# A softmax over 32768 columns: stores moved to ScalarE's queue, fixed buffers and a hand-written order

## The chip, the cores and the metric

The kernel runs on one core of one Trainium2 chip. The metric is the time of one execution on the device, in microseconds (us). Several executions of each kernel are timed and the median is given; one more execution is recorded by the hardware profiler, and all views of the profile are of that one. Names used below: VectorE is DVE in the profile, ScalarE is ACT, SyncE is SP (SPq where it issues transfers), GpSimd is POOL. TensorE has no work here.

## The reference

```python
def setup_inputs():
    batch, seq, vocab = 16, 256, 32768
    return {
        "logits": np.random.randn(batch, seq, vocab).astype(np.float32),
        "temperature": 1.0,
    }

def reference(logits, temperature):
    scaled = logits / temperature
    scaled = scaled - scaled.max(axis=-1, keepdims=True)
    exp_scaled = np.exp(scaled)
    return (exp_scaled / exp_scaled.sum(axis=-1, keepdims=True)).astype(np.float32)
```

It is a softmax over the last axis of a 4096 x 32768 float32 matrix. 536.87 MB are read and 536.87 MB are written, and each element needs to be read once and written once.

## The kernel before

Each of the 4096 rows is cut in two halves of 16384 columns (`_SPLIT = 2`), and each half is given a partition. A tile is therefore 128 partitions x 16384 float32: 64 rows of the matrix, 64 KB per partition, 8.39 MB. There are `G` = 64 tiles, contiguous in memory. `CW` equals the half row, so a tile is one chunk (`C` = 1) and the chunk index `i` is the tile index.

Three tile buffers (`_BUFS = 3`) come from a pool. For one tile the work is this:

- `load(i)`: SyncE issues a transfer from memory into the buffer. Tiles 0 and 63 are loaded in four transfers of 16 KB per partition, all others in one of 64 KB (line 64).
- `exps(i)`: for each of four pieces of 4096 columns, VectorE takes the negated maximum (line 107) and ScalarE computes Exp in place with that maximum as bias and a running sum (line 114).
- `factors(g)`: a few instructions on columns of 1 to 4 elements turn the four maxima and sums of each partition, and those of the partition with the other half of the same row (a shuffle, line 84), into one factor per piece (lines 129 to 150). They are marked as high priority.
- `scales(i)`: for each piece VectorE multiplies the first 2560 columns by the factor (line 160), and ScalarE multiplies the other 1536 (line 163).
- `store(i)`: SyncE issues the transfer back to memory, one of 64 KB per partition, or four of 16 KB for tile 63 (line 75).

All transfers thus go through one queue, SyncE's, and they are kept in program order. That order is written out by hand:

```python
    order = [("L", i) for i in range(min(_BUFS, n_chunks))] + [("S", 0)]
    for i in range(1, n_chunks):
        order.append(("S", i))
        if i + _BUFS - 1 < n_chunks:
            order.append(("L", i + _BUFS - 1))
```

SyncE's sequence is load 0, 1, 2, store 0, store 1, load 3, store 2, load 4, and so on. A store waits for the scaling of its tile by both engines. A load into a buffer waits for the store that empties it, and, because SyncE works in order, it also stands behind the store that precedes it in this sequence. A transfer is split over 16 DMA engines, 8 partitions to each, so that in a whole-tile transfer each engine moves eight rows of 64 KB.

Of the kernel before, what the change touches and what calls it, by code (L numbers as in the profile page):

```python
# [6 lines left out]


_SPLIT = 2
_CW = 16384  # L10
_BUFS = 3
_PIECE = 4096
_LAST_DMA = 4096
_DVE_SHARE = 0.625


@with_exitstack
def kernel(
    ctx: ExitStack,
    tc: tile.TileContext,  # L20
    logits: bass.AP,
    temperature: bass.AP,
    out: bass.AP,
):
    nc = tc.nc
    inv_t = 1.0 / float(temperature)
    P = nc.NUM_PARTITIONS
    fp32 = mybir.dt.float32
    Exp = mybir.ActivationFunctionType.Exp
    Copy = mybir.ActivationFunctionType.Copy  # L30
    X = mybir.AxisListType.X
    A = mybir.AluOpType

    xf = logits.flatten_outer_dims()
    of = out.flatten_outer_dims()
    N, V = xf.shape
    W = V // _SPLIT
    CW = min(_CW, W)
    C = W // CW
    assert W * _SPLIT == V and CW * C == W and (N * _SPLIT) % P == 0  # L40
    x = xf.rearrange("n (h v) -> (n h) v", h=_SPLIT)
    o = of.rearrange("n (h v) -> (n h) v", h=_SPLIT)
    G = N * _SPLIT // P
    n_chunks = G * C
    n_rounds = _SPLIT.bit_length() - 1

    xpool = ctx.enter_context(tc.tile_pool(name="x", bufs=_BUFS))
    spool = ctx.enter_context(tc.tile_pool(name="stats", bufs=3))
    slots = {}
    stats = {}  # L50

    def spans(total: int, step: int) -> list[tuple[int, int]]:
        return [(s, min(step, total - s)) for s in range(0, total, step)]

    def piece(g: int) -> int:
        return _PIECE if g < G - 1 else min(_PIECE, _LAST_DMA)

    def load(i: int) -> None:
        g, c = divmod(i, C)
        xs = xpool.tile([P, CW], fp32, tag="x", name="xs")  # L60
        slots[i] = xs
        for s, n in spans(CW, _LAST_DMA if g in (0, G - 1) else CW):
            tc.keep_in_program_order(
                nc.sync.dma_start(
                    out=xs[:, s : s + n],
                    in_=x[g * P : (g + 1) * P, c * CW + s : c * CW + s + n],
                )
            )

    def store(i: int) -> None:  # L70
        g, c = divmod(i, C)
        xs = slots.pop(i)
        for s, n in spans(CW, _LAST_DMA if g == G - 1 else CW):
            tc.keep_in_program_order(
                nc.sync.dma_start(  # L75
                    out=o[g * P : (g + 1) * P, c * CW + s : c * CW + s + n],
                    in_=xs[:, s : s + n],
                )
            )

    def combine(v, op) -> None:
        for j in range(n_rounds):
            mask = [i ^ (1 << j) for i in range(32)]
            nc.vector.stream_shuffle(  # L84
                out=v[:, j + 1 : j + 2], in_=v[:, j : j + 1], mask=mask
            )
            nc.vector.tensor_tensor(  # L87
                out=v[:, j + 1 : j + 2],
                in0=v[:, j : j + 1],
                in1=v[:, j + 1 : j + 2],  # L90
                op=op,
            )

    def exps(i: int) -> None:
        g, c = divmod(i, C)
        xs = slots[i]
        ps = spans(CW, piece(g))
        K = C * len(ps)
        if c == 0:
            stats[g] = tuple(  # L100
                spool.tile([P, K], fp32, tag=f"{nm}{K}", name=nm)
                for nm in ("nm", "ssum", "ee", "f", "ttj")
            )
        nm, ssum = stats[g][:2]
        for j, (s, n) in enumerate(ps):
            k = c * len(ps) + j
            nc.vector.tensor_reduce(  # L107
                out=nm[:, k : k + 1], in_=xs[:, s : s + n], axis=X, op=A.max, negate=True
            )
            if inv_t != 1.0:  # L110
                nc.vector.tensor_scalar_mul(
                    out=nm[:, k : k + 1], in0=nm[:, k : k + 1], scalar1=inv_t
                )
            nc.scalar.activation(  # L114
                out=xs[:, s : s + n],
                in_=xs[:, s : s + n],
                func=Exp,
                bias=nm[:, k : k + 1],
                scale=inv_t,
                accum_out=ssum[:, k : k + 1],  # L120
            )

    def factors(g: int) -> None:
        nm, ssum, ee, f, ttj = stats[g]
        nMh = spool.tile([P, 1 + n_rounds], fp32, tag="nMh", name="nMh")
        Sh = spool.tile([P, 1 + n_rounds], fp32, tag="Sh", name="Sh")
        rS = spool.tile([P, 1], fp32, tag="rS", name="rS")
        with tc.high_priority():
            nc.vector.tensor_reduce(out=nMh[:, 0:1], in_=nm, axis=X, op=A.min)  # L129
            combine(nMh, A.min)  # L130
            nc.scalar.activation(  # L131
                out=ee,
                in_=nm,
                func=Exp,
                bias=nMh[:, n_rounds : n_rounds + 1],
                scale=-1.0,
            )
            nc.vector.tensor_tensor_reduce(  # L138
                out=ttj,
                in0=ee,  # L140
                in1=ssum,
                scale=1.0,
                scalar=0.0,
                op0=A.mult,
                op1=A.add,
                accum_out=Sh[:, 0:1],
            )
            combine(Sh, A.add)
            nc.vector.reciprocal(out=rS, in_=Sh[:, n_rounds : n_rounds + 1])  # L149
            nc.vector.tensor_scalar_mul(out=f, in0=ee, scalar1=rS)  # L150

    def scales(i: int) -> None:
        g, c = divmod(i, C)
        xs = slots[i]
        f = stats[g][3]
        ps = spans(CW, piece(g))
        for j, (s, n) in enumerate(ps):
            k = c * len(ps) + j
            cut = int(n * _DVE_SHARE) // 512 * 512
            nc.vector.tensor_scalar_mul(  # L160
                out=xs[:, s : s + cut], in0=xs[:, s : s + cut], scalar1=f[:, k : k + 1]
            )
            nc.scalar.activation(  # L163
                out=xs[:, s + cut : s + n],
                in_=xs[:, s + cut : s + n],
                func=Copy,
                scale=f[:, k : k + 1],
            )

    order = [("L", i) for i in range(min(_BUFS, n_chunks))] + [("S", 0)]  # L170
    for i in range(1, n_chunks):
        order.append(("S", i))
        if i + _BUFS - 1 < n_chunks:
            order.append(("L", i + _BUFS - 1))

    nxt = 0
    done = -1
    loaded = 0
    for kind, i in order:
        if kind == "L":  # L180
            load(i)
            loaded = i + 1
        else:
            g = i // C
            if g > done:
                while nxt < (g + 1) * C:
                    assert nxt < loaded
                    exps(nxt)
                    nxt += 1
                factors(g)  # L190
                done = g
            scales(i)
            store(i)


# [33 lines left out]
```

## Time and profile before

| | |
|---|---|
| median of 8 runs | 2503.75 us (2497.48 to 2507.66) |
| the profiled execution | 2505.58 us, of which the span is 2503.8 us |
| VectorE busy | 1579.6 us (63%), 1216 instructions |
| ScalarE busy | 1368.8 us (55%), 833 instructions |
| DMA | 1073.91 MB in 19748 packets, mean 429 GB/s |
| maximum of 4096 columns, VectorE (line 107) | 256 times, mean 4412 ns |
| Exp of 4096 columns, ScalarE (line 114) | 256 times, mean 3708 ns |
| scaling, VectorE 2560 columns (line 160) | 256 times, mean 1549 ns |
| scaling, ScalarE 1536 columns (line 163) | 256 times, mean 1564 ns |

The span runs from the first to the last instruction in the trace. The busy shares are averages over it. "Issue to landing" of a transfer, used below, counts from the instruction that issues it to the moment its data are known to be there; it includes the time in which the transfer is queued behind others.

### The profile page before, as it was taken

How to read it: one execution, taken by the hardware profiler on the slowest of the kernel's cores; microseconds unless marked ns; L12 is line 12 of the kernel's file. 1: busy time of each engine (PE TensorE's matmuls, PEld its weight loads, DVE VectorE, ACT ScalarE, POOL GpSimd, SP SyncE). 2: the span in 40 equal slices, each digit the busy share in tenths (PEclk: the TensorE clock that was granted, in tenths of full speed). 3: DMA queues.
4: the chain of work that ended last, by engine and by line, in shares of the span. 5: the costliest groups of instructions: out<-in, count | busy, mean ns of one | idle time of the engine just before them, and what ended most of it. 6: DMA issues, size and time to landing. Idle time of an engine off the chain costs nothing.

```text
span 2503.8 us, 2498 instructions
## 1 busy us (share of the span) xinstructions
DVE 1579.6 (63%) x1216; ACT 1368.8 (55%) x833; POOL 0.2 (0%) x4
## 2 busy tenths in 40 slices
DVE  6575665765656657666575665766657566576665
ACT  5464554645546456465564655546556465564655
POOL 0000000000000000000000000000000000000000
DMA  9999999999999999999999999999999999999998
GB/s 419 434 427 428 435 433 435 435 436 431 436 436 435 429 434 429 435 434 433 433 423 433 424 431 433 424 421 436 429 425 433 431 423 435 420 435 432 423 425 376
DMA packets 19748, 1073.91 MB, mean 429 GB/s; under 512 B 2192, under 2 KB 2192, under 8 KB 2192
## 3 DMA queue, kind: packets, MB, share of 16 engines
q1 hardware_dynamic: 19728, 1073.75, 99.8%
q14 instruction: 20, 0.16, 0.0%
HBM read 536.87 MB, written 536.87 MB: 429 GB/s over the span
## 4 chain that ended last, share of the span: by engine, by line
DMA 71%; DVE 16%; ACT 10%; another core or an unknown queue 1%; SPq 1%; issue 0%; ACTq 0%
DMA xs<-in_logits_dram 69%; DVE nm L107 14%; ACT xs L163 7%; ACT xs L114 3%; DMA out_dram<-xs 2%; DVE xs L160 1%; SPq L75 1%; DVE f L150 0%; ACT ee L131 0%; DVE rS L149 0%; DVE Sh L87 0%; DVE Sh L84 0%; DVE ttj L138 0%; ACTq L224 0%
## 5 line engine op out<-in xcount | busy, mean ns | idle before, releaser
L107 DVE TENSOR_REDUCE nm<-xs 128x1 f32<-128x4096 f32 x256 | 1113.7, 4412 | 661.0 <-DMA xs<-in_logits_dram 661.0
L114 ACT ACTIVATE xs<-xs,nm 128x4096 f32<-128x4096 f32 x256 | 949.2, 3708 | 1032.1 <-DVE nm L107 1032.1
L163 ACT ACTIVATE xs<-xs,f 128x1536 f32<-128x1536 f32 x256 | 382.3, 1564 | 73.5 <-DVE f L150 73.5
L160 DVE TENSOR_SCALAR xs<-xs,f 128x2560 f32<-128x2560 f32 x256 | 380.2, 1549 | 2.6 <-DVE f L150 0.4
L138 DVE CUSTOM_DVE_ANT_0 ttj<-ee,ssum 128x4 f32<-128x4 f32 x64 | 10.4, 162 | 222.5 <-ACT ee L131 222.5
L114 ACT ACTIVATION_READ_ACCUMULATOR xs<-xs,nm 128x1 f32 x256 | 47.9, 187 | 0.0
L131 ACT ACTIVATE ee<-nm,nMh 128x4 f32<-128x4 f32 x64 | 18.0, 282 | 0.0
L150 DVE TENSOR_SCALAR f<-ee,rS 128x4 f32<-128x4 f32 x64 | 14.7, 229 | 2.2
L149 DVE RECIPROCAL rS<-Sh 128x1 f32<-128x1 f32 x64 | 10.5, 164 | 2.2
L87 DVE TENSOR_TENSOR nMh<-nMh 128x1 f32<-128x1 f32 x64 | 10.2, 159 | 2.2
L87 DVE TENSOR_TENSOR Sh<-Sh 128x1 f32<-128x1 f32 x64 | 10.2, 159 | 2.2
L129 DVE TENSOR_REDUCE nMh<-nm 128x1 f32<-128x4 f32 x64 | 10.0, 157 | 2.2
L84 DVE STREAM_SHUFFLE nMh<-nMh 128x1 f32<-128x1 f32 x64 | 9.7, 151 | 0.0
L84 DVE STREAM_SHUFFLE Sh<-Sh 128x1 f32<-128x1 f32 x64 | 9.7, 151 | 0.0
L114 ACT ACT_TABLE_LOAD x1 | 1.3, 1283 | 8.0 <-DMA xs<-in_logits_dram 8.0
L138 DVE DVE_READ_ACCUMULATOR2_ANT Sh<- 128x1 f32 x64 | 5.3, 82 | 0.0
L84 DVE LOAD_MASK_SELECT nMh<-nMh x64 | 0.9, 14 | 2.8
L84 DVE LOAD_MASK_SELECT Sh<-Sh x64 | 0.9, 14 | 2.8
L210 POOL MEMSET const-bfloat16-1.0<- 128x1 bf16 x1 | 0.1, 102 | 0.0
L210 POOL MEMSET const-uint8-127<- 128x1 uint8 x1 | 0.1, 102 | 0.0
L210 POOL MEMSET const-float32-0.0<- 128x1 f32 x1 | 0.1, 99 | 0.2 <-issue 0.2
L210 POOL MEMSET const-float32-1.0<- 128x1 f32 x1 | 0.1, 99 | 0.0
## 6 DMA issues: line engine op xcount, KB each, us to landing
xs<-in_logits_dram SPq DMA_DIRECT2D x8, 2048.0 KB, 27.6
out_dram<-xs SPq DMA_DIRECT2D x4, 2048.0 KB, 15.4
out_dram<-xs SPq DMA_DIRECT2D x63, 29.6
xs<-in_logits_dram SPq DMA_DIRECT2D x62, 49.2
```

The costliest lines, as they stand in the source:

```text
L75: nc.sync.dma_start(out=o[g * P : (g + 1) * P, c * CW + s : c * CW + s + n], in_=xs[:, s : s + n],)
L84: nc.vector.stream_shuffle(out=v[:, j + 1 : j + 2], in_=v[:, j : j + 1], mask=mask)
L87: nc.vector.tensor_tensor(out=v[:, j + 1 : j + 2], in0=v[:, j : j + 1], in1=v[:, j + 1 : j + 2], op=op,)
L107: nc.vector.tensor_reduce(out=nm[:, k : k + 1], in_=xs[:, s : s + n], axis=X, op=A.max, negate=True)
L114: nc.scalar.activation(out=xs[:, s : s + n], in_=xs[:, s : s + n], func=Exp, bias=nm[:, k : k + 1], scale=inv_t, accum_out=ssum[:, k : k + 1],
L129: nc.vector.tensor_reduce(out=nMh[:, 0:1], in_=nm, axis=X, op=A.min)
L131: nc.scalar.activation(out=ee, in_=nm, func=Exp, bias=nMh[:, n_rounds : n_rounds + 1], scale=-1.0,)
L138: nc.vector.tensor_tensor_reduce(out=ttj, in0=ee, in1=ssum, scale=1.0, scalar=0.0, op0=A.mult, op1=A.add, accum_out=Sh[:, 0:1],)
L149: nc.vector.reciprocal(out=rS, in_=Sh[:, n_rounds : n_rounds + 1])
L150: nc.vector.tensor_scalar_mul(out=f, in0=ee, scalar1=rS)
L160: nc.vector.tensor_scalar_mul(out=xs[:, s : s + cut], in0=xs[:, s : s + cut], scalar1=f[:, k : k + 1])
L163: nc.scalar.activation(out=xs[:, s + cut : s + n], in_=xs[:, s + cut : s + n], func=Copy, scale=f[:, k : k + 1],)
```

## The change

The kernel is written anew around the same arithmetic.

- The three tile buffers and three sets of small statistics tiles are allocated once and used in turn, tile `t` in buffer `t % 3`, in place of pools.
- Each engine executes its instructions in the order of the program (`tc.manual_schedule()`). The high-priority section is gone.
- Tiles 1 to 62 are computed in five pieces of 4096, 4096, 4096, 2048 and 2048 columns. VectorE scales 4096, 4096 and 2048 columns of the first three pieces, and ScalarE the remaining 2048 of the third and the last two pieces whole. Tiles 0 and 63 keep four pieces of 4096, with 2560 columns scaled by VectorE.
- Stores are issued by ScalarE, on its own queue: one transfer of 64 KB per partition after the scaling of a tile, and for tile 63 one of 16 KB per partition after each piece.
- Loads stay with SyncE. The load of tile `t + 3` follows the computation of tile `t` in the program, and waits for the store of tile `t`. Its size is `_LOAD` elements.

```diff
-_CW = 16384
 _BUFS = 3
-_PIECE = 4096
-_LAST_DMA = 4096
-_DVE_SHARE = 0.625
+_LOAD = 16384
+_PIECES = (4096, 4096, 4096, 2048, 2048)
+_ON_DVE = (4096, 4096, 2048, 0, 0)
+_END = 4096
+_END_ON_DVE = 2560
+_SETS = 3
...
+    pool = ctx.enter_context(tc.tile_pool(name="fixed", bufs=1))
+    buf = [pool.tile([P, W], fp32, tag=f"x{b}", name=f"x{b}") for b in range(_BUFS)]
...
+    def load(t: int) -> None:
+        n = _END if t in (0, G - 1) else _LOAD
+        for s in range(0, W, n):
+            nc.sync.dma_start(
+                out=buf[t % _BUFS][:, s : s + n],
+                in_=x[t * P : (t + 1) * P, s : s + n],
             )
...
-                nc.sync.dma_start(
-                    out=o[g * P : (g + 1) * P, c * CW + s : c * CW + s + n],
-                    in_=xs[:, s : s + n],
-                )
-            )
+    def store(t: int, a: int, b: int) -> None:
+        nc.scalar.dma_start(
+            out=o[t * P : (t + 1) * P, a:b], in_=buf[t % _BUFS][:, a:b]
+        )
...
+        for k in range(K):
+            a, b, c = at[k], at[k] + on_dve[k], at[k] + sizes[k]
+            if b > a:
+                nc.vector.tensor_scalar_mul(
+                    out=xs[:, a:b], in0=xs[:, a:b], scalar1=f[:, k : k + 1]
+                )
+            if c > b:
+                nc.scalar.activation(
+                    out=xs[:, b:c], in_=xs[:, b:c], func=Copy, scale=f[:, k : k + 1]
+                )
+            if t == G - 1:
+                store(t, a, c)
+        if t < G - 1:
+            store(t, 0, W)
...
-        with tc.high_priority():
-            nc.vector.tensor_reduce(out=nMh[:, 0:1], in_=nm, axis=X, op=A.min)
...
+    with tc.manual_schedule():
+        for t in range(_BUFS):
+            load(t)
+        for t in range(G):
+            normalise(t)
+            if t + _BUFS < G:
+                load(t + _BUFS)
```

The loop over pieces with the maxima and Exps, and the instructions for the factors, are the same as before with the new piece sizes and stand in `normalise(t)` in the same order.

## The prediction

> **What bounds the kernel now.** I read the page from the top: the DMA row and the rates under it, then the chain, the waits, SyncE's own waits, and last the timeline of SyncE's issues.
>
> ```profile
> DMA  9999999999999999999999999999999999999998
> GB/s 419 434 427 428 435 433 435 435 436 431 436 436 435 429 434 429 435 434 433 433 423 433 424 431 433 424 421 436 429 425 433 431 423 435 420 435 432 423 425 376
> ...
> q1 hardware_dynamic: 19728, 1073.75, 99.8%
> ...
> DMA 71%; DVE 16%; ACT 10%; another core or an unknown queue 1%; SPq 1%; issue 0%; ACTq 0%
> ...
> out_dram<-xs SPq DMA_DIRECT2D x63, 29.6
> xs<-in_logits_dram SPq DMA_DIRECT2D x62, 49.2
> ```
>
> The 16 DMA engines are busy for 99.8% of the span, all on one queue (q1, SyncE's). The best slices reach 436 GB/s, the worst in the middle 420; only the first and last are low for want of work. The chain is 71% DMA. So the bytes bound the kernel: 1073.74 MB, which the change does not touch. What can move is the rate at which they pass, and the two ends.
>
> ```profile
> DVE nm L107 <- DMA xs<-in_logits_dram: 661.0, 65, 22.9
> ```
>
> ```profile
> SPq L75 <- DVE xs L160: 2383.8, 67, 39.2
> ```
>
> VectorE waits 661 us for loads, so computing has room. SyncE stands 2383.8 us before its stores, waiting for VectorE's scaling; the next load is queued behind that wait. The waits end in time, because the queue holds work meanwhile:
>
> ```profile
> 385.63 0.33 SPq L75 DMA_DIRECT2D out_dram<-xs  x1
> 386.01 0.43 SPq L64 DMA_DIRECT2D xs<-in_logits_dram  x1
> 424.27 0.33 SPq L75 DMA_DIRECT2D out_dram<-xs  x1
> 424.65 0.43 SPq L64 DMA_DIRECT2D xs<-in_logits_dram  x1
> 462.93 0.33 SPq L75 DMA_DIRECT2D out_dram<-xs  x1
> ```
>
> Store and load go out as a pair, once a period. From the fourth store (150.25) to the last whole one (2454.01) are 59 periods in 2303.76 us, 39.05 us each. The shortest, and the commonest, is 38.63 us: two tiles of 8.39 MB at 434 GB/s. The other periods are up to 1.5 us longer. Over the 59 this costs 2303.8 - 59 x 38.63 = **24.6 us**, the only reserve inside the loop. The trace's packet records show where it lies: of the 16,000 rows of 64 KB, 95 in 100 took 2.415 to 2.427 us and none less; the slow ones, up to 3.9 us, sit almost all at the last or first row of a transfer, where an engine turns from loading to storing or back, and they come in clusters of engines that turn at the same moment. With two turns a period, 24.6 us is 0.21 us per turn. In the calm stretch from 501.83 to 1006.56 us the period is 504.73 / 13 = 38.83 us, 0.10 us per turn. Elsewhere engines are up to 3 rows apart, so that some load while others store, and rows in the middle of a transfer keep 2.418 us: mixed directions across engines cost nothing here.
>
> [...] The trace before has one queue; it shows that the time to be saved is small (0.33 us a store). [...]
>
> **The change, part by part.**
>
> *Load size.* The words speak of 32 KB loads, but `_LOAD` is 16384 float32, the whole 64 KB row. The loads stay what they were, 4 of 16 KB at tiles 0 and 63, one transfer elsewhere: 0 us. That part of the description is not in the kernel.
>
> *Fixed buffers, program order.* Three tiles, as before, and tile by tile, as the traced order already is: 0 us.
>
> *Pieces 4096, 4096, 4096, 2048, 2048.* From landing to store issue is 28.6 us now (200.87 to 229.44). The maxima remain 16384 columns, 4 x 4.35 = 17.4 us; the last Exp is half as wide (3.71 to about 1.9 us) but stands behind one more Exp, one more accumulator read (0.19) and a gap of 0.5. Scaling stays 10240 columns on VectorE (now 5.94 us in four, 2.48 + 2.48 + 1.24 = 6.2 by the same rate) and 6144 on ScalarE. Sum: -0.5 to +0.5 us a tile, covered by VectorE's 10 us of waiting a tile (661 / 65): 0 us. If that cover were gone, 64 x 0.5 = 32 us either way.
>
> *Store issue on ScalarE.* 67 issues of 0.33 us, 22 us, leave SyncE for ScalarE. Each waits there for VectorE's last scaling, which ends within 0.3 us of ScalarE's own. Behind it stand the next tile's Exps, which need a maximum first (4.41 us), and ScalarE waits 1032 us for those: hidden, 0 us. If ScalarE's issue took 2 us it would still fit.
>
> *Loads freed.* A load now waits only for the store of its own buffer to land. A store lands 29.6 us after issue, the next pair goes at 38.7, so on SyncE loads could go some 9 us sooner. Engines that are never idle can't use it: 0 us.
>
> *Two rings.* With both filled, each transfer gets half the rate, 38.6 us. A buffer's round is then 38.6 + 28.6 + 38.6 and some 6 us of latencies [...], 111.8 us, against 3 x 38.63 = 115.9. It closes with 4 us to spare; if it didn't, one ring would run alone at full rate, so the loss is 0 to some 5 us. What remains is the price of turns, not shown for two rings. From below: if engines cease to turn all together, the excess goes, -24.6 us and not more, since no row is under 2.415. From above: if engines alternate row by row, 16 turns a period take the place of 2.
>
> *Ends.* Head: 150 us to the fourth store, rings full, 0 to -1. Tail: 49.8 us from the last whole store on, made of VectorE's serial 28.8 us and four 16 KB-row stores; same chain, four issues on ScalarE of which one counts: 0 to +4 us.
>
> Sum: I take the calm stretch's rate for the loop, 59 x (39.05 - 38.83) = -13 us, and nothing else. The profiled execution took 2505.58 us (span 2503.8, 1.8 around it), which gives 2492.5; it lies 1.8 above the median of 2503.75, so in terms of the median **2491 us**.
>
> **The rivals.** About 0.2%, 5 us, is what a measurement of this kernel can tell from no change.
>
> *A, turns no longer collective (0.42).* Each engine is fed from either ring, and the 16 drift apart. For it: rows amid mixed directions keep 2.418 us; the clusters vanish almost wholly between 500 and 1000 us. Against: the reserve is 1%. Time 2479 to 2498, I take 2491.
>
> *B, whole transfers in turn (0.18).* An engine drains its 8 rows of one transfer and then turns, as the single queue does now. Two turns a period, the same excess: 2504, from 2499 to 2509. [...] Against: even so the moments of turning would shift.
>
> *C, row by row (0.40).* Place: the change of direction inside each engine, 16 a period. It decides from 24.6 / (59 x 16) = 0.026 us per turn on; above that the kernel is slower. At the calm stretch's 0.10 us it is 2479 + 94 = 2573; at the mean 0.21, 2479 + 198 = 2677. I give it 2545[...]. For it: turns are the only slow rows in the trace. Against: many turns there cost nothing.
>
> *D, ScalarE held up by its store waits* is bounded above at some 0.3 us a tile, hidden; it has no chance of its own.
>
> **How the numbers follow.** Faster is A, same is B, slower is C: 0.42, 0.18, 0.40. Likeliest is A, 2491, with its own range 2479 to 2498. The range for all reaches from 2481 over B into C, up to the calm price, 2575; some 0.15 is left above and a little below.
>
> **What would show it.** Right under A: loads on q1, stores on a second queue; DMA share as before; middle slices at 434 to 436; store issues 38.6 to 38.8 us apart; loads and stores about 40 us from issue to landing. B: landings near 20 us plus waiting, slices as uneven as now. C: an even rate under 425 in all middle slices at 99% share. Wrong altogether: DMA tenths under 9 in the middle, or ScalarE waits that end at a store.

## The result and the profile after

The changed kernel takes 2514.99 us, median of 11 executions (2512.25 to 2516.86). The kernel before, run beside it, takes 2502.55 us, median of 32 (2494.75 to 2509.05). The ratio is **1.0052** with a 95% interval of 1.0041 to 1.0063: slower by half a per cent, 13 us. The forecast was 2491 us. The profiled execution took 2514.64 us with a span of 2512.9 us, which is 9.1 us more than the span before. Between the medians it is 12.4 us; most of the rest is that the profiled execution before lies 3.0 us above its own median.

The first view is the page of the kernel after: the rates in 40 slices, the queues, the wait of VectorE for loads, and the transfers with the median time from issue to landing.

```profile
DMA  9999999999999999999999999999999999999996
GB/s 404 392 427 434 435 433 435 434 434 434 434 432 431 434 427 433 434 434 429 434 435 435 435 435 432 436 432 426 433 433 431 433 431 429 433 434 433 433 427 295
...
q1 hardware_dynamic: 10080, 536.88, 49.7%
q10 hardware_dynamic: 9648, 536.88, 49.5%
...
L99 DVE TENSOR_REDUCE nm<-x 128x1 f32<-128x4096 f32 x318 | 1117.6, 3580 | 703.8 <-DMA x<-in_logits_dram 703.8
...
out_dram<-x ACTq DMA_DIRECT2D x63, 44.4
x<-in_logits_dram SPq DMA_DIRECT2D x62, 43.5
```

Loads (q1) and stores (q10), the two rings of this text, share the engines half and half (49.7 and 49.5%), and the two kinds of transfer now take the same 44 us, where they took 49.2 and 29.6. Of the 37 slices in the middle 28 stand at 432 or more, against 20 before. The first two and the last are what has become worse: 404 and 392 instead of 419 and 434, and 295 instead of 376.

The windows show it by stage. The columns are the stretch, its length, the busy time and instructions of VectorE, ScalarE and GpSimd, the clock, the DMA share and GB/s. The kernel before:

```profile
40.00:80.00 40.00, 34.22 (x22) 26.02 (x16) 0.00 (x0) 1.00 1.00 419
80.00:120.00 40.00, 15.05 (x17) 16.71 (x11) 0.00 (x0) 1.00 1.00 429
120.00:160.00 40.00, 24.68 (x19) 21.37 (x13) 0.00 (x0) 1.00 1.01 434
...
200.00:2400.00 2200.00, 1396.01 (x1068) 1204.98 (x733) 0.00 (x0) 1.00 1.00 431
...
2460.00:2480.00 20.00, 16.23 (x17) 17.28 (x12) 0.00 (x0) 1.00 0.87 376
2480.00:2504.00 24.00, 2.25 (x2) 2.34 (x2) 0.00 (x0) 1.00 0.79 336
```

The kernel after:

```profile
40.00:80.00 40.00, 24.62 (x19) 21.35 (x14) 0.00 (x0) 1.00 0.98 365
80.00:120.00 40.00, 24.61 (x19) 21.35 (x14) 0.00 (x0) 1.00 0.97 405
120.00:160.00 40.00, 20.91 (x17) 17.61 (x13) 0.00 (x0) 1.00 1.01 438
...
200.00:2400.00 2200.00, 1394.79 (x1070) 1206.54 (x790) 0.00 (x0) 1.00 1.00 433
...
2460.00:2480.00 20.00, 3.65 (x2) 6.59 (x4) 0.00 (x0) 1.00 0.64 279
2480.00:2513.00 33.00, 11.33 (x16) 10.29 (x7) 0.00 (x0) 1.00 0.60 254
```

From 200 to 2400 us the rate is 433 GB/s, against 431 before in the same window. From 40 to 80 us it is 365 GB/s at a DMA share of 0.98 (before: 419): the engines have work and are slow. From 40 to 160 us the kernel after falls (54 + 24 - 4) GB/s x 40 us = 3.0 MB behind, which is 7 us at 434 GB/s. From 2460 us on the share is 0.6 (before: 0.87 and 0.79): the engines have too little work. So the two ends fail in different ways.

The store issues divide the span. I use the fourth store, the last whole store and the end.

| us | before | after | difference |
|---|---|---|---|
| head, to the fourth store | 150.25 | 163.8 | +13.5 |
| loop, 59 periods | 2303.76 (39.05 each) | 2286.6 (38.76 each) | -17.2 |
| tail, from the last whole store | 49.8 | 62.5 | +12.7 |
| span | 2503.8 | 2512.9 | +9.1 |

These three differences add up by construction, and the border between head and loop misleads. When the fourth store is issued, the packet records of the kernel after have 66.1 MB moved, those of the kernel before 63.4. So 2.7 MB, some 6 us, of the 13.5 us are work that is already done and that the loop doesn't need to do. In terms of bytes the head lost about 7 us and the loop won about 11.

Nor is the loop's gain the second ring's alone. Executions of the kernel before lie up to 14 us apart, and the same rewrite with one queue (experiment 1) has a period of 38.92 us in its profile, 7.8 us less than the kernel before over 59 periods. **The tail lost 12.7 us and the head about 7; the loop won about 11, of which these profiles put some 3 us to the second ring.** The experiments give a better figure for the last: with both ends repaired, about 5 us are left (experiment 8).

The tail is seen in the timeline of the kernel after (start, duration, engine, line, instruction; in brackets the idle time before it and what ended it).

```profile
2454.54 8.74 DVE L99 TENSOR_REDUCE nm<-x 128x1 f32<-128x4096 f32 x2
...
2479.63 4.42 DVE L99 TENSOR_REDUCE nm<-x 128x1 f32<-128x4096 f32 x1 [16.35 <-DMA x<-in_logits_dram]
...
2490.97 0.34 ACTq L68 DMA_DIRECT2D out_dram<-x  x1
...
2496.95 0.34 ACTq L68 DMA_DIRECT2D out_dram<-x  x1
```

The second and third maximum of the last tile run back to back from 2454.54 us. The fourth piece is there only at 2479.63, after 16.35 us of waiting. The kernel before takes all four maxima of its last tile in one go, from 2453.80 to 2471.19 us, and its last piece store goes out at about 2482.5, 14 us sooner.

The packet records say why. By 2460.4 us every engine but one has started its last row of load 63. That one is behind, and it shares its time with store 62, issued at 2450.38. These are its records, from my reading of the trace (start in us, duration in ns, bytes, queue; q1 loads, q10 stores). A record doesn't name its engine; I put those together where one starts as another ends.

```
2455.26 2418 65536 q10
2457.68  611 16384 q1
2458.28 2418 65536 q10
2460.70  611 16384 q1
2461.30 2418 65536 q10
2463.72  611 16384 q1
2464.33 2418 65536 q10
2466.74  611 16384 q1
```

The engine takes one row from each ring in turn. A row of the last load is 16 KB (0.61 us) and a row of the store is 64 KB (2.42 us), so the load, on which all the remaining computation depends, gets a fifth of the engine. Its rows start 3.02 to 3.33 us apart, and it goes on so until 2476.2. With one queue, load 63 stood ahead of store 62 and was done before it: in the records of the kernel before its last row starts at 2463.2 us, and the last row of store 62 ends at 2483.2. Why that engine is behind is not shown; the same wait, of 16.1 and 16.3 us, stands in head_fifo12 and head_only below.

### The profile page after: what moved, and what is told of

Read it like the earlier page. It is cut to its first block, busy times and chain, and to the rows that moved or that the text cites. A ratio compares the mean times of both kernels' runs of the same rounds, so it can differ in the third digit from the quotient of the medians.

```text
span 2512.9 us, 2617 instructions
## 1 busy us (share of the span) xinstructions
DVE 1575.8 (63%) x1216; ACT 1368.1 (54%) x895; POOL 0.2 (0%) x4
## 3 DMA queue, kind: packets, MB, share of 16 engines
q1 hardware_dynamic: 10080, 536.88, 49.7%
q10 hardware_dynamic: 9648, 536.88, 49.5%
## 4 chain that ended last, share of the span: by engine, by line
DMA 72%; DVE 17%; ACT 9%; another core or an unknown queue 1%; issue 0%; SPq 0%; ACTq 0%
DMA x<-in_logits_dram 36%; DMA out_dram<-x 36%; DVE nm L99 12%; ACT x L106 7%; DVE x L135 4%; ACT x L139 2%; DVE f L131 0%; ACT ee L116 0%; DVE rS L130 0%; DVE Sh L78 0%; DVE ttj L119 0%; DVE Sh L75 0%; SPq L62 0%; ACTq L68 0%
## 5 line engine op out<-in xcount | busy, mean ns | idle before, releaser
L99 DVE TENSOR_REDUCE nm<-x 128x1 f32<-128x4096 f32 x318 | 1117.6, 3580 | 703.8 <-DMA x<-in_logits_dram 703.8
L106 ACT ACTIVATE x<-x,nm 128x4096 f32<-128x4096 f32 x318 | 965.4, 3036 | 1045.7 <-DVE nm L99 1045.7
L139 ACT ACTIVATE x<-x,f 128x2048 f32<-128x2048 f32 (+1 forms) x194 | 371.2, 1975 | 75.1 <-DVE f L131 73.7
L135 DVE TENSOR_SCALAR x<-x,f 128x4096 f32<-128x4096 f32 (+2 forms) x194 | 372.2, 1975 | 2.5 <-DVE f L131 0.2
L119 DVE CUSTOM_DVE_ANT_0 ttj<-ee,ssum 128x5 f32<-128x5 f32 (+1 forms) x64 | 10.6, 165 | 196.7 <-ACT ee L116 196.7
L106 ACT ACTIVATION_READ_ACCUMULATOR x<-x,nm 128x1 f32 x318 | 59.3, 186 | 0.0
L116 ACT ACTIVATE ee<-nm,nMh 128x5 f32<-128x5 f32 (+1 forms) x64 | 18.1, 284 | 0.0
L131 DVE TENSOR_SCALAR f<-ee,rS 128x5 f32<-128x5 f32 (+1 forms) x64 | 14.8, 231 | 2.2
L114 DVE TENSOR_REDUCE nMh<-nm 128x1 f32<-128x5 f32 (+1 forms) x64 | 10.1, 158 | 2.2
```

Of the source, the lines that this page charges most:

```text
L99: nc.vector.tensor_reduce(out=nm[:, k : k + 1], in_=xc, axis=X, op=A.max, negate=True)
L106: nc.scalar.activation(out=xc, in_=xc, func=Exp, bias=nm[:, k : k + 1], scale=inv_t, accum_out=ssum[:, k : k + 1],)
L116: nc.scalar.activation(out=ee, in_=nm, func=Exp, bias=nMh[:, n_rounds : n_rounds + 1], scale=-1.0)
L119: nc.vector.tensor_tensor_reduce(out=ttj, in0=ee, in1=ssum, scale=1.0, scalar=0.0, op0=A.mult, op1=A.add, accum_out=Sh[:, 0:1],)
L135: nc.vector.tensor_scalar_mul(out=xs[:, a:b], in0=xs[:, a:b], scalar1=f[:, k : k + 1])
L139: nc.scalar.activation(out=xs[:, b:c], in_=xs[:, b:c], func=Copy, scale=f[:, k : k + 1])
```

## The experiments

All ratios are to the kernel before, run beside each on the same chip, with 95% intervals. "Slow time" below is worked out from the packet records: what the rows of 64 KB took above 2.418 us and those of 16 KB above 0.611 us, summed over the first 160 us and divided by the 16 engines. It is 7.8 us in the kernel after.

### 1. The rewrite with one queue (one_queue)

```diff
+_FIFO = 64
...
-        nc.scalar.dma_start(
+        (nc.sync if t < _FIFO else nc.scalar).dma_start(
```

The loads are also put back into the order of the kernel before (store 0, store 1, load 3, store 2, load 4, and so on). Everything else of the rewrite stays.

> The changed kernel with all stores back on SyncE's queue and in the order of the kernel before (store 0, store 1, load 3, store 2, load 4, ...); buffers, pieces and hand-written order stay as changed. Theory (the second ring alone matters; the rest of the rewrite is worth nothing): 2503 us like the kernel before, within 5 us, fourth store issued near 150 us, mean period near 39.05 us, about 50 us from the last whole store to the end. Rival (the rewrite of pieces and order costs the time): it stays near 2515 us.

Measured: 2498.89 us, ratio 0.9996 (0.9986 to 1.0007). Slow time 2.4 us, tail 51.5 us. Fixed buffers, the program order and the five pieces are worth nothing that can be measured; the whole loss belongs to the second ring, with the order of loads that goes with it.

### 2 and 3. Another shape of the last load (tail_64k, tail_part)

```diff
-        n = _END if t in (0, G - 1) else _LOAD
+        n = _END if t == 0 else _LOAD
```

> The changed kernel with the last tile loaded in one transfer of 64 KB rows instead of four of 16 KB rows. Theory (engines take turns row by row between the two rings, so a 16 KB row gets a fifth of the rate beside 64 KB rows and the last tile lands late): the last tile lands before VectorE is free for it, the 16 us wait for it goes, from the last whole store to the end 50 us instead of 62.5, time about 2502 to 2504 us. Rival (the last load is late because it is issued late, after store 60 has landed): no change, 2515 us.

Measured: 2511.28 us, ratio 1.0042 (1.0027 to 1.0057). The wait for the last load falls from 16.3 to 11.5 us and the tail from 62.5 to 57.5 us. With rows of equal size the load does get half of each engine, and its last row starts at 2458.3 us instead of 2476.2. But the tile now comes as a whole, so the first maximum has to wait as well:

```profile
2463.60 17.40 DVE L99 TENSOR_REDUCE nm<-x 128x1 f32<-128x4096 f32 x4 [11.50 <-DMA x<-in_logits_dram]
```

That took back most of it. The expectation overlooked that the four pieces also serve to start the maxima early.

In tail_part the last tile is loaded in four transfers of 32 partitions, with rows of 64 KB:

```diff
+        if t == G - 1:
+            for p in range(0, P, 32):
+                nc.sync.dma_start(
+                    out=buf[t % _BUFS][p : p + 32, :],
+                    in_=x[t * P + p : t * P + p + 32, :],
+                )
+            return
```

> The changed kernel with the last tile still loaded in four transfers, but each of 32 partitions with whole 64 KB rows. Theory (the size of the row decides, not the number of transfers): the same as with one transfer, 2502 to 2504 us. Rival (four transfers in place of one, with their issue and landing, make it late): near 2515 us.

Measured: 2537.27 us, ratio 1.0163 (1.0123 to 1.0202). It decides nothing: rows of 64 KB took about 4.4 us there instead of 2.418, and VectorE waited 34.3 us for them. Transfers over a quarter of the partitions brought a cost of their own.

### 4. The last two stores back on SyncE's queue (tail_sp)

```diff
-        nc.scalar.dma_start(
+        (nc.sync if t >= G - 2 else nc.scalar).dma_start(
```

Tiles 62 and 63 are stored on the queue of the loads, behind load 63.

> The changed kernel with the stores of the last two tiles on SyncE's queue, behind the last load, which keeps its four transfers of 16 KB rows. Theory (the last load's leftover rows, on an engine that lags, take turns with the rows of store 62, 3.0 us each instead of 0.6): store 62 now stands behind them on the same queue, the 16 us wait of VectorE for the last piece goes, and from the last whole store to the end it is 50 us instead of 62.5; about 2503 us. Rival (the lagging engine is late for another reason): still some 16 us of waiting, 2515 us.

Measured: 2502.37 us, ratio 1.0006 (0.9994 to 1.0017). From the timeline of this kernel:

```profile
2449.29 17.39 DVE L99 TENSOR_REDUCE nm<-x 128x1 f32<-128x4096 f32 x4
2449.44 28.87 SPq L68 DMA_DIRECT2D out_dram<-x  x5
```

The four maxima run without a gap, all five last transfers go out from SyncE within 28.87 us, and the tail is 50.0 us, as it was before the change. The 12.6 us of the tail are thus the last load's share beside store 62, and two stores on the other queue give them back.

### 5. One queue for the first twelve tiles (head_fifo12)

As in one_queue, with `_FIFO = 12`: only stores from tile 12 on go to ScalarE's ring.

> The changed kernel with the stores of tiles 0 to 11 on SyncE's queue, in the order of the kernel before, and those from tile 12 on ScalarE's queue. Theory (alternating row by row is dear only while the 16 engines turn in step, which they do at the start and no longer after some 500 us): fourth store issued near 150 us instead of 163.8, then periods of 38.6 to 38.8 us without a cluster of slow rows where the second ring begins, about 2500 to 2502 us. Rival (a ring that begins is dear whenever it begins): slow rows of some 8 us in total after store 12, about 2508 us or more.

Measured: 2517.23 us, ratio 1.0067 (1.0051 to 1.0083). The head was good (slices of 417 and 433), but where the second ring came in, near 500 us, some 8.5 us were lost all the same: store issues there are 46.3 and 45.0 us apart in places instead of 38.6, with 5.0 us of slow time and 3.4 us of idle engines between 500 and 700 us. So a loss comes with the entry of the second ring in mid-run too, as the rival of this expectation had it. My premise that the engines would be well apart by then was weak: 7 of the 16 were still within 0.2 of a row, and another 6 in a second group.

### 6. Is it that all engines turn in step? (stagger, stagger_ctl)

At the start of the slow stretch, near 50 us, all 16 engines change direction at the same moments: 16 load rows start from 46.75 to 47.44 us, 16 store rows from 49.28 to 49.85. Three small extra loads, over 12, 8 and 4 partitions, ought to spread them; the control has 16 partitions in each, meant to be the same for all engines. The data land in a tile that is loaded afterwards.

```diff
+_SHIFT = (12, 8, 4)
...
+        for j, k in enumerate(_SHIFT):
+            c = j * 4096
+            nc.sync.dma_start(out=buf[2][0:k, c : c + 4096], in_=x[0:k, c : c + 4096])
```

> The changed kernel with three extra small loads of 16 KB rows after load 0, over 12, 8 and 4 partitions, whose data are overwritten by load 2: they delay some of the 16 DMA engines by one, two or three rows of 0.6 us, so that groups of four engines instead of all 16 should turn at one moment when the first store joins. Theory (rows at a turn are slow because all engines turn in step): the slow rows of the first 160 us, 7 us per engine in the changed kernel, fall to some 2 us, the fourth store is issued 5 us sooner, about 2510 us. Rival (the cost of two rings beginning does not hang on the step): the same 7 us, 2515 us or, with the extra loads, up to 2517.

> As the staggered one, but each of the three extra loads is over 16 partitions, one row for every engine, so that no engine is moved against another. Both theories: as the changed kernel plus up to 2 us, 2515 to 2517 us, 7 us of slow rows in the first 160 us.

Measured: 2524.48 us, 1.0098 (1.0081 to 1.0116), and 2524.85 us, 1.0099 (1.0082 to 1.0117). The two do not differ, so the theory of the common turn falls. The extra loads cost about 5 us themselves. In both, the slow rows vanish from 40 to 80 us and come back from 80 to 160 us (7.6 and 7.8 us), in the first while the engines are spread evenly. With tail_sp added (stagger_tail, 2510.51 us, 1.0053, 1.0031 to 1.0075) the tail's gain is there, and the slow rows come back as well (5.0 us).

> The changed kernel with the three extra loads over 12, 8 and 4 partitions and with the stores of the last two tiles on SyncE's queue. If both theories hold the gains add: 2515 - 12 - 5 = 2498 us. If only that of the tail holds, 2503 us.

What the slow stretches have in common is another thing. A tile gives each engine eight rows, one per partition (16,000 rows of 64 KB in 125 transfers, over 16 engines). I count the rows begun by loads and those begun by stores, as a mean over the 16 engines; their difference modulo 8 says how many rows the store is behind the load. In the kernel after this is 0.0 to 1.0 rows from 42 to 80 us. From 50 us on, load rows took 0.45 to 0.74 us too long there and store rows 0.14 to 0.33 (means over 10 us). In the loop it is 5.1 to 7.9 rows, and 96 of 100 rows take 2.418 us. The runs with extra loads fit: stagger has about 5 rows and no slow row from 40 to 80 us, and under one row, with load rows 0.5 to 1.0 us too long, from 90 to 128 us. This gave a new theory: alternation is free, unless load and store stand at **the same row of their tiles**.

### 7. The first store a little later (s0_late1, s0_late2, s0_late4)

If the row distance decides, then a later first store must help, because store 0 then meets load 2 at another row. The kernels are tail_sp with two, four or nine extra instructions on ScalarE before store 0; their result goes to a tile that nobody reads.

```diff
+_LATE = 9
...
+    junk = pool.tile([P, 1024], fp32, tag="junk", name="junk")
...
+            if t == 0:
+                for _ in range(_LATE):
+                    nc.scalar.activation(
+                        out=junk, in_=xs[:, W - 1024 : W], func=Copy, scale=1.0
+                    )
```

> The changed kernel with the stores of the last two tiles on SyncE, and with two Copy instructions of 1024 columns ahead of the first store, some 2.3 us, about one row. Theory (slow rows come where an engine alternates between equal row numbers of load and store, and one row apart is already enough): slow rows of the first 160 us near 1 us per engine, as with two rows, 2498 us. Rival (the effect fades only with distance): between 7.4 and 1.3 us of slow rows, about 2500 us. Other rival (nothing but the start of the second ring): 7 us, 2502 us.

> The changed kernel with the stores of the last two tiles on SyncE, and with four Copy instructions of 1024 columns into an unused tile on ScalarE ahead of the first store only, so that this store is issued some 4.5 us later. Theory (rows are slow while each engine alternates between the same row number of a load and of a store, as it does when the first store and load 2 begin together; rows that are several numbers apart are not slow): the first store now runs some two rows behind load 2, the slow rows of the first 160 us fall from 7.4 us per engine to under 4, and the time from 2502 to about 2498 us. Rival (two rings are slow whenever the second begins): still 7 us of slow rows, 2502 us or up to 4 us more for the later store.

> The same with nine such instructions, some 10 us, four rows. Theory: slow rows of the first 100 us under 2 us per engine, about 2496 us. Rival: 7 us of slow rows as before, 2502 to 2512 us.

| kernel | store 0 issued | rows apart while store 0 and load 2 alternate | slow time | us | ratio (95%) |
|---|---|---|---|---|---|
| tail_sp | 38.2 | 0.0 to 1.0 | 8.0 | 2502.37 | 1.0006 (0.9994 to 1.0017) |
| s0_late1 | 39.7 | 0.0 to 1.0 | 8.1 | 2501.26 | 1.0001 (0.9991 to 1.0012) |
| s0_late2 | 41.5 | 1.0 to 2.0 | 1.8 | 2498.13 | 0.9992 (0.9982 to 1.0002) |
| s0_late4 | 47.0 | 3.0 to 4.3 | 2.1 | 2495.35 | 0.9986 (0.9967 to 1.0004) |

The 1.5 us of s0_late1 were too little to move store 0 to another row: its distance did not rise above one, and slow time did not fall. I had counted the delay as one row, and that expectation failed for this reason. As a control it says that a delay alone does nothing. With one to two rows the slow rows are all but gone. The times of neighbours in this table overlap; what separates the kernels is the slow time, and the comparison of s0_late4_again with tail_sp below. The windows of s0_late4 show it, to be set beside those of the kernel after:

```profile
40.00:80.00 40.00, 30.33 (x21) 30.14 (x23) 0.00 (x0) 1.00 0.99 419
80.00:120.00 40.00, 18.89 (x18) 20.09 (x14) 0.00 (x0) 1.00 1.02 438
```

419 and 438 GB/s stand where there were 365 and 405. Third and fourth store are issued at 102.34 and 151.87 us, instead of 119.06 and 163.79.

### 8. The head alone, and the whole repair again (head_only, s0_late4_again)

head_only is the changed kernel with the nine instructions and nothing done to the tail.

> The changed kernel with nine such instructions ahead of the first store and nothing else changed: all stores stay on ScalarE, the tail as it was. Theory (head and tail are separate losses): slow rows of the first 160 us fall to about 1.5 us, the tail keeps its 16 us of waiting for the last piece; 2515 - 7 = 2508 us.

Measured: 2509.18 us, ratio 1.0033 (1.0022 to 1.0045). The fourth store comes at 151.4 us and slow time is 2.0 us. The tail's loss is still there, in the waits of its last 100 us (engine, line, what it waited for; total, times, longest):

```profile
DVE nm L101 <- DMA x<-in_logits_dram: 27.0, 2, 16.3
```

So the two losses are separate: the head's repair is worth about 6 us by the medians, the tail's 12.6 (2514.99 to 2502.37; by the ratios 4.8 and 11.5), and together they should give about 2496. The 6 us agree with the 7 us of bytes above and not with the 13.5 us of the store issues.

> The kernel with both repairs once more (first store some 10 us later, last two stores on SyncE), for a sharper comparison with the kernel before: 2495 us, ratio 0.998, with an interval below 1 if the gain is real.

Measured: 2496.77 us (22 executions) against 2501.95, ratio **0.9979** (0.9970 to 0.9988). The kernel with both repairs is faster than the kernel before, by about 5 us, and than the changed kernel by 18. With the ends no worse than before, these 5 us are what the rewrite and the second ring bring over the whole loop; the rewrite with one queue alone, at 0.9996, shows no gain.

### 9. The same offset, forced in the loop (loop_late3, loop_late6)

tail_sp with three or five of the same instructions before each store from tile 3 to tile 59.

```diff
+_LATE = 5
...
+            if 3 <= t < G - 4:
+                for _ in range(_LATE):
```

> The changed kernel with the stores of the last two tiles on SyncE, and with three Copy instructions of 1024 columns ahead of the store of every tile from 3 to 59, some 3.4 us on ScalarE, which is idle for more than 15 us a tile. In the loop a store begins some 6 us ahead of the next load, so that their rows are about two numbers apart; this brings them to about one apart. Theory: slow rows appear in the loop, some 0.1 to 0.5 us a row, the period goes from 38.7 to 39.5 us or more, 2540 us or more. Rival (only a ring's beginning is slow, and a late store is covered by the other ring): period 38.7, 2502 us.

> The same with five such instructions, some 5.7 us, so that store and next load begin together and run at the same row number. Theory: slow rows all through the loop, up to the 0.45 us a row of the first 90 us, which is 7 us a tile; period over 40 us, 2600 us or more. Rival: period 38.7, 2502 us, as 29 + 6 us of computing still fit in the period.

Measured: 2513.02 us, 1.006 (1.0035 to 1.0086), and 2545.03 us, 1.0164 (1.0133 to 1.0194). The direction is that of the theory, the sizes are not (2540 and 2600 or more were expected): the distance did not settle at zero, and for nine tenths of loop_late6's loop it was 6 to 8 rows. The time did go into slow rows. From 200 to 2400 us their slow time is 21 and 39 us, against 5 us in tail_sp, while the idle time of the engines grew by 5 and 7 us. So the buffer's round, which the delay of 5.7 us brings by estimate from 111.8 to 117.5 us (39.2 us a period), is not what mainly holds loop_late6 back, although it shows 39.3 us. But in loop_late6 22 of the 39 us fall where the distance is 7 to 8 rows, and almost all of that on store rows (0.3 us each), where tail_sp has the same distance for an eighth of its loop and 0.05 us. So these two don't bear out the row theory as it stands.

## Why the prediction was wrong

- **What bounds the kernel** was right. The bytes and the rate at which they pass set the loop before and after, and VectorE still waits 703.8 us in all for loads.
- **Load size, fixed buffers, pieces, program order: 0 us.** Right: one_queue is at 0.9996. The loads are 62 transfers of 64 KB a partition, as the prediction read from `_LOAD`.
- **Store issue on ScalarE: 0 us.** Right as to the issue itself, 0.34 us each, and no listed wait of ScalarE ends at a store. What SyncE saves is as small as the prediction had it (67 issues of 0.34 us). What another engine also brings here is another ring (q10), and by one_queue that ring is the whole 0.5%.
- **Two rings, the loop: -13 us.** Right in sign, too large in size. The pair of profiles shows about -11 us in bytes, but 7.8 us less than before also stand in the loop of one_queue's profile, with one queue. The medians with both ends repaired give -5 us (interval -7.5 to -3). The 39.05 us a period from which the prediction counted were those of one execution that lay above its median. The buffer's round, reckoned at 111.8 us against 115.9, did close: the DMA share is 1.00 from 200 to 2400 us. The 6 us of latencies in it were the author's estimate. A landing itself came only 0.38 to 0.47 us after the last row (the four pieces of load 0 in the kernel before).
- **Rivals B and C.** The engines turn row by row: C's mechanism, not B's. The trace has one record for each row, of 64 KB or of 16 KB. With the records put together into engines as above, from 200 to 2400 us 79 of 100 rows follow one of the other ring. With three to five of the other transfer's eight rows begun it is 99.8 of 100; the repeats stand almost all near the ends of a transfer, and no more than five rows of one ring come in succession. A turn after a whole transfer of eight rows, as B had it, is ruled out. B was an assumption: the trace before has one queue and could not show how two are served. But C's price, 0.10 to 0.21 us a turn in 16 turns, was wrong, and the 2545 us given to C, less than this price makes, had no measured basis. The price came from turns of one queue from load to store; in the loop with two rings, 96 of 100 rows keep 2.418 us although four in five are turns (7 us of slow time in all from 200 to 2400 us). The loop thus went as in A by C's mechanism, at a price of almost nothing.
- **Ends.** This is the step that failed: "Head: 150 us to the fourth store, rings full, 0 to -1. Tail: [...] same chain, four issues on ScalarE of which one counts: 0 to +4 us." Measured: the tail +12.7 us, the head +13.5 us to the fourth store, of which about 7 us are lost time.
  - *The tail.* The chain was taken as the same because the same instructions stand in it. Whether its first member, load 63, still goes ahead of store 62 was not asked. In one queue the order gave load 63 priority; in two rings the size of its rows took it away. The numbers were at hand: 16 KB beside 64 KB is 0.61 + 2.42 = 3.03 us a row, and this load is the last that anybody waits for. tail_sp shows that it is this.
  - *The head.* "Rings full" was true (share 0.98), and full was taken for fast. The statement behind it, that mixed directions cost nothing, was taken from engines that differ in direction from each other. That one engine alternating between load and store would run at full speed was an assumption, and near 40 to 100 us it does not (load rows 0.45 to 0.92 us too long, means over 10 us). s0_late1, s0_late2 and s0_late4 show that, for this stretch, the row at which store 0 meets load 2 decides (slow time 8.1 us at 0.0 to 1.0 rows, 1.8 at 1.0 to 2.0).
- **The sum.** From the experiments it is -5 us for the loop, +6 us for the head and +12.6 us for the tail, 13.6 us, against 12.4 us between the medians; so the two repairs add up. The prediction had -13 for the loop and nothing for the ends. No rival held this case, a loop that wins a little and ends that lose more; 2515 us lies in the range for all cases only because that range joins B and C.

**What stays open.** Why equal row numbers are slow is not shown. By the kernel's addressing, load and store at the same row have the same partition of their buffers, and also the same offset within a tile in the device's memory; whether either is the cause, no run here tells. It wasn't tried, because transfers over other partitions change the time of a row (4.4 us in tail_part). The reading is good for the long slow stretches only. There were short bursts at other distances (in the kernel after, 16 load rows took 0.92 us too long from 90 to 100 us, at 4.2 to 6.2 rows; in head_fifo12, 671 to 679 us at six to seven rows; of its 5.0 us of slow time after 500 us only 1.7 us lie at distances under two rows, so its loss is mostly unexplained). The profiled execution of s0_late4_again, its slowest (2504.2 us), has rows that are on average up to 0.12 us too long between 250 and 600 us, at six to eight rows. And the slow store rows of loop_late6 stand at seven to eight.

## What to carry to other kernels

Putting loads and stores on two rings trades an order that is written down for a share by row sizes (0.61 us in 3.03 for the last load): look at each place where one transfer is urgent (here the last load), and keep it and what may stand in its way on one ring, which gave back the whole tail here; rows as large as its neighbour's (tail_64k) gave back 5 of the 12.7 us. Cost the ends by themselves, with the row times from the trace, because the 5 us that two rings won over this whole loop were lost more than three times over there. Compare two kernels at points where they have moved the same bytes, and not only at the same instruction. And when engines are fully busy but below their rate, look in the packet records at which rows meet; here 3.3 us of delay at one issue were enough.

## What the runs showed of the hardware

- An engine with work on two rings took one row from each in turn (99.8 of 100 rows with three to five of the other transfer's eight begun, kernel after, 200 to 2400 us). In its tail a 16 KB row waited each time for a 64 KB row of the other ring: 3.02 to 3.33 us apart instead of 0.61.
- Alternating between loading and storing, at 79 of 100 rows, cost almost nothing in the loop of the kernel after, with the store 5.1 to 7.9 rows behind the load (2.418 us for 96 of 100 rows), and 0.45 to 0.74 us per load row and 0.14 to 0.33 us per store row from 50 to 80 us, with less than one row between them. With store 0 one to two rows behind, in s0_late2, the slow rows of that stretch were all but gone (0.02 us a load row).
- Rows of 64 KB in transfers over 32 partitions took about 4.4 us instead of 2.418 (tail_part). Rows of 16 KB in transfers over at most 16 partitions took up to 2.4 us instead of 0.611 (stagger_ctl), and the first 64 KB rows behind them up to 7.4 us (stagger).
